# Hybrid streaming trunk on one core: the merge's weights split in two turns, in the middle of the second group's channel jobs

## The chip, the cores and the metric

One core of a Trainium2 chip runs the whole program. The metric is the device time of one execution in microseconds. The kernel before takes 2898.13 us in the median of three runs (2896.23 to 2900.97).

## The reference, cut to what matters

The reference is one step of an encoder layer over 2048 prompt rows and 8 x 16 sample rows, 17 tiles of 128 rows in all. Each row is normalised, h = RMSNorm(x), and multiplied by one wide input projection; its columns feed three branches (a gated convolution, a gated linear recurrence, a stick-breaking attention) and three sigmoid gates. Each branch's output is projected to 1024 columns, the three results are added with the gates as weights, and the sum goes through one output projection onto the residual.

```python
h = rms_norm(x, norm_g[l])
(a_x, a_b, a_c, a_z, g_q, g_f, g_i, g_z,
 s_q, s_k, s_v, s_z, m_a, m_b, m_c) = split_cols(h @ w_in[l])
...
y_a = o_a @ wb[:W_CONV]
y_b = o_b @ wb[W_CONV:W_CONV + W_HG]
y_c = o_c @ wb[W_CONV + W_HG:]
m = jax.nn.sigmoid(m_a) * y_a + jax.nn.sigmoid(m_b) * y_b + jax.nn.sigmoid(m_c) * y_c
return x + m @ w_out[l], conv_new, S_new.astype(x.dtype), k, v
```

Everything is float32.

## The kernel before, in words

Big products are done in three passes: a float32 operand is split into a rounded part and the rest (`split`, lines 173 to 176: a copy on ScalarE writes the rounded part, a subtraction on VectorE the rest), and high times high, high times low and low times high are added in PSUM. A weight that is used again is kept split in DRAM (`kept`), so that it is only loaded the next time (`wload`).

The rows go through the input projection in three groups (`GROUPS`: 5, 6 and 6 tiles), each of two chunks of up to three tiles. `group_jobs` makes a list of jobs for a group, 64 in the second and third. A channel job (`chan_job`, line 710) computes 128 output columns for a whole chunk, 24 matmuls of 384 columns, and hands the running program a turn after every six. A token job (`tok_job`, line 721) does 256 columns for each tile; keys, values and queries (`sk`, `sv`, `sq`) and the recurrence's `gi` are of this kind. `run_jobs` takes the jobs of a group in an order of pairs (job, chunk): in the second and third group it begins with jobs 0 and 1 on the first chunk, then jobs 0 and 1 on the second chunk, and goes on chunk by chunk; the position in this order is `at_`, from 0 to 127. Keys, values and queries take up the even jobs 2 to 12, that is positions up to 25.

Between the turns of a job `run_jobs` lets other work go on: the preparation of rows (`Prepare`), what is left of the norms of queries and keys (`run_late`), the recurrence (`hbg`) and the attention (`bg`). `Prepare` brings a tile of 128 rows into the transposed and split form that the matmuls read (`hx`), in steps: the load on the SyncE queue (line 607, 512 KB), the square with its sum on ScalarE (line 614), a power on GpSimd, the scaling on VectorE (line 619), and two turns of four transposes on TensorE (line 629), each followed by `split`. The tiles of rows have two buffers (`xt`) and a third for one of them (`xt3`). In the last group the sixth tile takes the buffer of the fourth, so its load has to wait until the fourth is transposed. `prep.advance()` does one step; `prep.chunk(ci)` does all steps up to the last tile of a chunk before a job on that chunk begins. Before the change, the first two jobs of every group (positions 0 and 1) make two steps in each of their turns, so the second chunk's rows are made while the first chunk's matmuls run.

The weights of the merge (12 pieces of the branch projections and 8 of the output projection) are split by the generator `split_merge_weights` while the second group runs, in 40 halves of 128 x 512. A half is a load into `mwx`, a split into `mwp` and a store to DRAM; each of the two tiles has one buffer. Before the change one of these three steps is made at the beginning of each position from 4 to 123.

What the Python code writes is not yet the order on the engines. The framework schedules the instructions and puts each into its engine's queue (TensorE, VectorE, ScalarE, GpSimd, and SyncE for all transfers); each engine takes its queue in order. An instruction can so be placed well ahead of others that the code writes earlier. A transfer also waits for the eighth transfer before it on the queue to be complete, since there are eight completion counters in turn.

Of the kernel before, what the change touches and what calls it, by code (L numbers as in the profile page):

```python
# [8 lines left out]
F32 = mybir.dt.float32  # L9
# [7 lines left out]
P = 128  # L17
# [81 lines left out]
def trunk(ctx: ExitStack, tc: tile.TileContext, x_prompt, x_sample, cache_conv, state_hgrn, cache_k, cache_v,  # L99
# [73 lines left out]
    def split(hi, lo, src, eng=None):  # L173

        first = nc.scalar.copy(hi, src)  # L175
        return first, (eng or nc.vector).tensor_tensor(lo, src, hi.bitcast(F32), ALU.subtract)  # L176
# [1097 lines left out]
    def branch_w(x, dp):  # L1274
        return ([wb[x * 512:(x + 1) * 512, dp * 256:(dp + 1) * 256].rearrange("(k p) m -> p k m", p=P)],
                ("branch", x, dp))

    def out_w(s):
        v = wo[:, s * 256:(s + 1) * 256].rearrange("(k p) m -> p k m", p=P)
        return [v[:, 0:4], v[:, 4:8]], ("out", s)  # L1280

    def split_merge_weights():

        mw = mwx.enter_context(tc.tile_pool(name="mw", bufs=1, side="right"))
        yield
        for pieces, key in [branch_w(x, dp) for x in range(3) for dp in range(4)] + [out_w(s) for s in range(4)]:
            for n, v in enumerate(pieces):
                kept[key, n] = dram.tile([P, 2, 1024], F32R, name=f"W{len(kept)}")
                a, b = v.shape[1], v.shape[2]
                for half in range(2):  # L1290
                    x = mw.tile([P, 512], F32, tag="mwx", name="mwx")
                    nc.sync.dma_start(x.rearrange("p (a b) -> p a b", b=b), v[:, half * a // 2:(half + 1) * a // 2])
                    yield
                    w = mw.tile([P, 2, 512], F32R, tag="mwp", name="mwp")
                    split(w[:, 0], w[:, 1], x)
                    yield
                    nc.sync.dma_start(kept[key, n][:, :, half * 512:(half + 1) * 512].bitcast(F32), w.bitcast(F32))
                    yield

    splitting = split_merge_weights()  # L1300

    def run_jobs(g, jobs):
# [13 lines left out]
        for at_, (i, ci) in enumerate(order):  # L1316
            weights(i)
            if g or at_:
                weights(i + 1)
            if g == 1 and 4 <= at_ < len(order) - 4:  # L1320
                next(splitting, None)
            if not g and at_ == 0:
                prep.advance()
            if not g and at_ == 2:

                with tc.issue_after(rstd_at[0].ins), tc.issue_after(prep.last[1].ins):
                    build_vectors()
                    build_hist()
                    build_rev()
                    build_bound()  # L1330
                    build_masks()
                    build_selectors()
            hT = prep.chunk(ci) if g or at_ > 1 else lambda ti, ci=ci: prep.tile(ci, ti)
            left = len(order) - at_
            if left == 5 and g + 1 < len(GROUPS):
                nxt = Prepare(g + 1)
            for cost in jobs[i][1](ws[i], ci, hT):
                if at_ < 2:
                    prep.advance()
                    prep.advance()  # L1340
                if nxt and (left <= 2 or nxt.ready < 0 and len(nxt.xt) < 3 or left <= 3 and not nxt.scaled):
                    nxt.advance()
                run_late(cost)
                hbg.run(cost * RATE_H)
                bg.run(cost * RATES[g] * jobs[i][2])
            if ci == 0 and g < len(GROUPS) - 1:
                wkeep(ws[i], jobs[i][0][1])
# [164 lines left out]
```

## Time and profile before

| | |
|---|---|
| median of 3 runs | 2898.13 us |
| profiled execution | 2896.27 us |
| its span | 2894.6 us |
| TensorE matmul busy | 2864.3 us, 99% of the span |
| VectorE, ScalarE, GpSimd busy | 1547.5, 1025.5, 317.0 us |
| second group begins | about 588 us |
| third group begins | about 1355 us |
| splits of the merge's weights | 584.0 to 1090.3 us |

The span is what lies between the first and the last instruction of the execution. A matmul counts as busy until its modelled end, and matmuls overlap, so the busy share of TensorE hides short delays; a delay is read from the start of one matmul to the start of the next. In rows of the timeline the bracket at the end gives the idle time of the engine before the instruction and what ended it. In rows of windows the columns are the window, its length, then the busy time and the number of instructions of TensorE's matmuls, its weight loads, VectorE, ScalarE and GpSimd, then the granted clock of TensorE (1.00 is 2.4 GHz, 0.50 is 1.2 GHz), the share of the transfer engines and the rate in GB/s.

### The profile page before, as it was taken

Reading aid. Unit: us, or ns where it says so; the run is one execution under the profiler, and the core shown is the slowest. Engines: PE = TensorE matmul, PEld = TensorE weight load, DVE = VectorE, ACT = ScalarE, POOL = GpSimd, SP = SyncE. Lnnn points to the kernel's source line nnn. Section 1 sums busy time; section 2 is a strip of 40 time slices with the busy share of each in tenths; the row PEclk is TensorE's granted clock in tenths of the full one; section 3 lists DMA queues with packets and bytes.
Section 4 is the critical chain, followed back from the end, with each engine's and each line's share of the span. In section 5 each row is a group of like instructions: output and inputs, shape, how many; then the busy total and the mean of one; then the engine's idle time right before and its main releaser. Section 6 shows DMA issues by size and latency. Waiting matters only on the chain.

```text
span 2894.6 us, 51726 instructions
## 1 busy us (share of the span) xinstructions
PE 2864.3 (99%) x19511; PEld 2671.5 (92%) x19511; DVE 1547.5 (53%) x3304; ACT 1025.5 (35%) x2391; POOL 317.0 (11%) x787
## 2 busy tenths in 40 slices
PE   9999999999999999999999999999999999999999
PEld 9999999989899999999999999999988888788888
DVE  5454645642334351526534757547475875867743
ACT  4333222242333332213334444434433444444420
POOL 3100000110100000001322111010110111110100
PEclk9999999999999999999999999999999999999999
DMA  8987767788777786446776454444446877878876
GB/s 306 310 262 241 242 219 246 245 266 289 247 246 255 258 262 202 152 138 185 218 231 206 140 178 131 161 139 150 146 138 222 293 241 233 262 251 265 271 251 223
DMA packets 367403, 645.57 MB, mean 223 GB/s; under 512 B 32969, under 2 KB 243746, under 8 KB 336434
## 3 DMA queue, kind: packets, MB, share of 16 engines
q1 hardware_dynamic: 367154, 642.26, 67.7%
q8 instruction: 155, 2.54, 0.4%
q14 instruction: 94, 0.77, 0.1%
HBM read 444.97 MB, written 197.17 MB: 222 GB/s over the span
## 4 chain that ended last, share of the span: by engine, by line
PE 73%; DMA 3%; DVE 3%; issue 1%; ACT 1%; POOL 1%; SPq 0%; ACTq 0%; DVEq 0%; POOLq 0%
PE acc L710 31%; PE acc L1420 10%; PE acc L721 8%; PE acc L1451 7%; PE pv L359 4%; PE tp L310 4%; PE z L330 2%; PE z L329 2%; DMA mwx<-in_w_branch_dram 1%; PE z L1040 1%; PE tp L458 1%; DMA mwx<-in_w_out_dram 1%; PE pv L522 1%; DMA GM<-gm 0%; PE z L476 0%
## 5 line engine op out<-in xcount | busy, mean ns | idle before, releaser
L710 PE MATMUL acc<-hx,w 128*128 128x384 f32 (+1 forms) x6816 | 1254.3, 333 | 0.1
L710 PEld LDWEIGHTS acc<-hx,w 128*128 128x128 f32 x6816 | 1107.4, 188 | 22.1 <-issue 15.2
L721 PE MATMUL acc<-w,hx 128*128 128x256 f32 x2544 | 330.3, 285 | 2.9 <-ACT kn L815 1.3
L342 DVE TENSOR_TENSOR_SCAN pr<-snb,carry 128x513 f32<-128x513 f32 x192 | 246.5, 1284 | 152.2 <-ACT snb L333 150.6
L721 PEld LDWEIGHTS acc<-w,hx 128*128 128x128 f32 x2544 | 312.4, 189 | 6.0 <-ACT kn L815 2.2
L311 ACT COPY aT<-tp 128x512 f32<-128x512 f32 (+2 forms) x320 | 167.7, 525 | 370.4 <-PE tp L310 357.5
L710 PE MATMUL acc<-hx,wst 128*128 128x384 f32 x1248 | 247.3, 344 | 0.0
L1420 PE MATMUL acc<-o,w 128*128 128x512 f32 (+2 forms) x1080 | 234.6, 363 | 1.1 <-DMA o<-OX 1.1
L333 ACT ACTIVATE snb<-z 128x512 f32<-128x512 f32 (+2 forms) x320 | 172.4, 539 | 144.3 <-PE z L330 140.7
L710 PEld LDWEIGHTS acc<-hx,wst 128*128 128x128 f32 x1248 | 215.5, 188 | 6.4 <-issue 3.7
L1420 PEld LDWEIGHTS acc<-o,w 128*128 128x128 f32 x1080 | 184.9, 188 | 33.0 <-issue 4.5
L347 DVE TENSOR_TENSOR sp<-sp,pr 128x512 f32<-128x512 f32 (+2 forms) x320 | 195.4, 611 | 26.7 <-DVE pr L342 1.0
L342 DVE TENSOR_TENSOR_SCAN pr<-snb,one 128x129 f32<-128x129 f32 (+3 forms) x128 | 114.5, 895 | 126.4 <-POOL snb L338 126.1
L310 PE MATMUL tp<-idf,sp 128*128 128x128 f32 x1088 | 171.3, 273 | 2.6 <-ACT aT L311 1.6
L335 ACT ACTIVATE sp<-z 128x512 f32<-128x512 f32 (+2 forms) x320 | 171.4, 536 | 0.0
L1451 PE MATMUL acc<-w,mh 128*128 128x256 f32 x816 | 160.5, 284 | 0.0
L310 PEld LDWEIGHTS tp<-idf,sp 128*128 128x128 f32 x1088 | 131.9, 141 | 19.6 <-issue 4.4
L176 DVE TENSOR_TENSOR w<-wst,w 128x1024 fp32r<-128x1024 f32 x72 | 88.1, 1224 | 106.3 <-ACT w L175 106.2
L1174 ACT ACTIVATE gm<-acc 128x384 f32<-128x384 f32 (+1 forms) x144 | 68.3, 474 | 213.8 <-PE acc L710 181.3
L1451 PEld LDWEIGHTS acc<-w,mh 128*128 128x128 f32 x816 | 130.7, 188 | 5.8 <-issue 4.2
L329 PE MATMUL z<-Kt,Q 128*128 128x512 f32 (+2 forms) x320 | 129.2, 404 | 0.4 <-ACT sp L335 0.2
L359 PE MATMUL pv<-aT,Vt 128*64 128x512 f32 (+3 forms) x640 | 128.1, 535 | 0.0
(302 smaller groups left out, 3581.5 us busy)
## 6 DMA issues: line engine op xcount, KB each, us to landing
w<-W SPq DMA_DIRECT2D x168, 1024.0 KB, 6.3
W<-w SPq DMA_DIRECT2D x72, 1024.0 KB, 5.0
wst<-W SPq DMA_DIRECT2D x112, 512.0 KB, 5.0
wst<-in_w_in_dram SPq DMA_DIRECT2D x72, 512.0 KB, 6.0
GM<-gm SPq DMA_DIRECT2D x120, 192.0 KB, 4.1
W<-mwp SPq DMA_DIRECT2D x40, 512.0 KB, 4.3
Kt<-KT SPq DMA_DIRECT2D x160, 128.0 KB, 3.9
o<-OX SPq DMA_DIRECT2D x72, 256.0 KB, 4.7
```

What stands on the lines that cost most here:

```text
L310: nc.tensor.transpose(tp[:, j * P:(j + 1) * P], sp[:, j * P:(j + 1) * P], idf)
L311: nc.scalar.copy(aT[:, e, 0:nb, i * P:(i + 1) * P], tp[:, :w].rearrange("p (b q) -> p b q", q=P))
L329: nc.tensor.matmul(z[:, :w], Q1[:, i * P:(i + 1) * P], Kt[:, :w], start=True, stop=False)
L333: nc.scalar.activation(sn[:, 512 - w:512], z[:, :w], AF.Sigmoid, scale=-0.125)
L335: nc.scalar.activation(sp[:, :w], z[:, :w], AF.Sigmoid, scale=0.125)
L342: nc.vector.tensor_tensor_scan(pr[:, 512 - w:513][:, ::-1], s_in, s_in, one if diag else carry[e][i], ALU.mult, ALU.bypass)
L347: nc.vector.tensor_tensor(sp[:, :w], sp[:, :w], pr[:, 513 - w:513], ALU.mult)
L359: nc.tensor.matmul(pv[64 * e:64 * e + 64, c0:n], Vt[:, j, e], aT[:, e, j, c0:n], start=first and j == 0, stop=last and j == nb - 1, skip_g ...
L710: nc.tensor.matmul(acc[:, :n], w[0][a][:, k], hT[b][:, k, :n], start=k == 0 and i == 0, stop=k == KB - 1 and i == 2)
L721: nc.tensor.matmul(acc[:, :256], hT[b][:, k, ti * P:(ti + 1) * P], w[k // 4][a][:, k % 4], start=k == 0 and i == 0, stop=k == KB - 1 and i ...
L1420: nc.tensor.matmul(acc[:, :n], w[0][a][:, k, dd * P:(dd + 1) * P], box[x][b][:, k, sl], start=k == 0 and i == 0, stop=k == 3 and i == 2)
L1451: nc.tensor.matmul(acc[:, :256], box["l" if b else "h"][:, k, ti * P:(ti + 1) * P], w[k // 4][a][:, k % 4], start=k == 0 and i == 0, stop= ...
```

## The change

The generator now makes a half in two turns: the first stores the half split before and loads the next one, the second splits. `run_jobs` calls it no longer at the beginning of a position but behind the second turn of a channel job (`jobs[i][2] == 1.0`) of the second group, from position 26 on, which is behind the jobs of keys, values and queries. There are 96 such places for 80 turns and the last store. One line beside it changes too: the two steps of `prep.advance()` in each turn of positions 0 and 1 are now made in the first group alone (`and not g`).

```diff
--- before.py
+++ after.py
@@ -1283,19 +1283,26 @@
 
         mw = mwx.enter_context(tc.tile_pool(name="mw", bufs=1, side="right"))
         yield
+        halves = []
         for pieces, key in [branch_w(x, dp) for x in range(3) for dp in range(4)] + [out_w(s) for s in range(4)]:
             for n, v in enumerate(pieces):
                 kept[key, n] = dram.tile([P, 2, 1024], F32R, name=f"W{len(kept)}")
-                a, b = v.shape[1], v.shape[2]
-                for half in range(2):
-                    x = mw.tile([P, 512], F32, tag="mwx", name="mwx")
-                    nc.sync.dma_start(x.rearrange("p (a b) -> p a b", b=b), v[:, half * a // 2:(half + 1) * a // 2])
-                    yield
-                    w = mw.tile([P, 2, 512], F32R, tag="mwp", name="mwp")
-                    split(w[:, 0], w[:, 1], x)
-                    yield
-                    nc.sync.dma_start(kept[key, n][:, :, half * 512:(half + 1) * 512].bitcast(F32), w.bitcast(F32))
-                    yield
+                a = v.shape[1] // 2
+                halves += [(v[:, half * a:(half + 1) * a], kept[key, n][:, :, half * 512:(half + 1) * 512])
+                           for half in range(2)]
+        made = None
+        for src, dst in halves + [(None, None)]:
+            if made:
+                nc.sync.dma_start(made[0].bitcast(F32), made[1].bitcast(F32))
+            if src is None:
+                return
+            x = mw.tile([P, 512], F32, tag="mwx", name="mwx")
+            nc.sync.dma_start(x.rearrange("p (a b) -> p a b", b=src.shape[2]), src)
+            yield
+            w = mw.tile([P, 2, 512], F32R, tag="mwp", name="mwp")
+            split(w[:, 0], w[:, 1], x)
+            made = (dst, w)
+            yield
 
     splitting = split_merge_weights()
 
@@ -1317,8 +1324,8 @@
             weights(i)
             if g or at_:
                 weights(i + 1)
-            if g == 1 and 4 <= at_ < len(order) - 4:
-                next(splitting, None)
+
+            extra = g == 1 and 26 <= at_ < len(order) - 2 and jobs[i][2] == 1.0
             if not g and at_ == 0:
                 prep.advance()
             if not g and at_ == 2:
@@ -1334,8 +1341,10 @@
             left = len(order) - at_
             if left == 5 and g + 1 < len(GROUPS):
                 nxt = Prepare(g + 1)
-            for cost in jobs[i][1](ws[i], ci, hT):
-                if at_ < 2:
+            for turn_, cost in enumerate(jobs[i][1](ws[i], ci, hT)):
+                if extra and turn_ == 1:
+                    next(splitting, None)
+                if at_ < 2 and not g:
                     prep.advance()
                     prep.advance()
                 if nxt and (left <= 2 or nxt.ready < 0 and len(nxt.xt) < 3 or left <= 3 and not nxt.scaled):
```

What this does to the queues shows at three places. The first is TensorE at the beginning of the third group, where the second chunk's rows (tiles `xt_15317`, `xt_15376` and a last one, 15472 before and 15631 now) are transposed; `acc_15458` and `acc_15598` (15553 now) are the first two jobs on the first chunk, `acc_15669` is the first job on the second chunk, and `z` are scores of the attention's first heads. Before:

```order
L710 MATMUL acc_15458<-hx_15272,w_15454 128x384 x6
L629 MATMUL tp_15465<-idf_79,xt_15317 128x128 x4
L710 MATMUL acc_15458<-hx_15272,w_15454 128x384 x12
L629 MATMUL tp_15535<-idf_79,xt_15376 128x128 x4
L710 MATMUL acc_15458<-hx_15272,w_15454 128x384
L629 MATMUL tp_15548<-idf_79,xt_15376 128x128 x4
L710 MATMUL acc_15458<-hx_15272,w_15454 128x384 x5
L710 MATMUL acc_15598<-hx_15272,w_15456 128x384 x16
L629 MATMUL tp_15555<-idf_79,xt_15472 128x128 x4
L629 MATMUL tp_15581<-idf_79,xt_15472 128x128
```

Now:

```order
L710 MATMUL acc_15553<-hx_15272,w_15456 128x384 x3
L629 MATMUL tp_15624<-idf_79,xt_15317 128x128 x4
L629 MATMUL tp_15641<-idf_79,xt_15376 128x128 x4
L329 MATMUL z_15607<-Kt_15482,Q1_15476 128x128
L330 MATMUL z_15607<-Kt_15482,Q2_15477 128x128
L329 MATMUL z_15686<-Kt_15482,Q1_15476 128x256
L629 MATMUL tp_15648<-idf_79,xt_15376 128x128 x4
L330 MATMUL z_15686<-Kt_15482,Q2_15477 128x256
L329 MATMUL z_15716<-Kt_15482,Q1_15476 128x384
L330 MATMUL z_15716<-Kt_15482,Q2_15477 128x384
L629 MATMUL tp_15655<-idf_79,xt_15631 128x128 x4
L629 MATMUL tp_15662<-idf_79,xt_15631 128x128 x4
```

The transposes stood between matmuls of the first chunk; now they stand behind the last of them, together, with scores between, and directly ahead of the second chunk's first matmuls.

The second place is SyncE's queue in the same stretch. Before, the last tile of rows was loaded behind the first of the attention's transfers:

```order
L1175 DMA GM_77<-gm_15431 128x384
L281 DMA Q1_15481<-QT_73 64x512
L282 DMA Q2_15482<-QT_73 64x512
L607 DMA xt_15472<-in_x_prompt_dram 128x1024
L281 DMA Q1_15481<-QT_73 64x512
L282 DMA Q2_15482<-QT_73 64x512
L287 DMA Kt_15487<-KT_72 64x512 x2
L291 DMA Vt_15490<-VV_74 128x4x128
```

Now its load stands behind three sets of them, the last of which is for the third head, and behind the store of a gate (`gm_15620`):

```order
L281 DMA Q1_15594<-QT_73 64x512
L282 DMA Q2_15595<-QT_73 64x512
L281 DMA Q1_15594<-QT_73 64x512
L282 DMA Q2_15595<-QT_73 64x512
L287 DMA Kt_15600<-KT_72 64x512 x2
L291 DMA Vt_15603<-VV_74 128x4x128
L320 DMA ot_15605<-SZ_76 128x512
L1183 DMA SZ_76<-gm_15620 128x384
L607 DMA xt_15631<-in_x_prompt_dram 128x1024
```

The load has moved back by twenty places in the queue.

The third place is ScalarE at the beginning of the second group. `hx_6983` is the second chunk's rows, `xt_15094` and `xt_15109` are the first rows of the third group, which the scheduler fetches as soon as a buffer is free, `mwp` are halves of the merge's weights, and `sq` and `kn` further down belong to the first job of keys. Before:

```order
L175 CAST hx_6983<-tp_6998 128x4x128
L175 CAST hx_6983<-tp_7039 128x4x128
L175 CAST hx_6983<-tp_7046 128x4x128
L614 ACTIVATE junk_6975,ssq_6976<-xt3_6973 128x1024
L459 COPY kt_7059<-tp_7062 128x4x128
L1133 ACTIVATE gm_7094<-acc_6991 128x384
L175 CAST hx_6983<-tp_7074 128x4x128
L175 CAST hx_6983<-tp_7081 128x4x128
L175 CAST mwp_7635<-mwx_7573 128x512
```

Now:

```order
L175 CAST hx_6983<-tp_7120 128x4x128
L175 CAST hx_6983<-tp_7128 128x4x128
L175 CAST hx_6983<-tp_7135 128x4x128
L175 CAST mwp_9691<-mwx_9639 128x512
L175 CAST hx_6983<-tp_7142 128x4x128
L614 ACTIVATE junk_15096,ssq_15097<-xt_15094 128x1024
L175 CAST hx_6983<-tp_7149 128x4x128
L614 ACTIVATE junk_15111,ssq_15112<-xt_15109 128x1024
```

The square of `xt_15094` stood behind all casts of the second chunk's rows; now it stands ahead of the last of them. In VectorE's queue the scaling of `xt_15094` has likewise come to stand ahead of the last subtraction of `hx_6983`. A little later, in the first job of keys, ScalarE's queue had:

```order
L813 ACTIVATE sq_7315<-acc_7290 128x256
L815 COPY kn_7317<-acc_7290 128x256
L175 CAST mwp_8247<-mwx_8152 128x512
L813 ACTIVATE sq_7353<-acc_7325 128x256
L815 COPY kn_7355<-acc_7325 128x256
L614 ACTIVATE junk_15137,ssq_15138<-xt3_15135 128x1024
```

and has now:

```order
L813 ACTIVATE sq_7312<-acc_7287 128x256
L815 COPY kn_7314<-acc_7287 128x256
L175 CAST mwp_9914<-mwx_9842 128x512
L813 ACTIVATE sq_7350<-acc_7322 128x256
L815 COPY kn_7352<-acc_7322 128x256
```

A cast of the merge's weights (`mwp`) stands behind the second `kn` of the keys' job in both, although the code now writes it only from position 26 on; the square of `xt3_15135`, a row tile of the third group, has left this stretch. Behind these two stretches, at the beginnings of the second and the third group, the queues of all five engines read the same before and after.

## Rows read from the trace of the kernel before

**Rows 1.** The page's busy times: time, share of the span and number of instructions of each engine.

```profile
PE 2864.3 (99%) x19511; PEld 2671.5 (92%) x19511; DVE 1547.5 (53%) x3304; ACT 1025.5 (35%) x2391; POOL 317.0 (11%) x787
```

**Rows 2.** Windows of 50 us in which TensorE is not busy throughout.

```profile
600.00:650.00 50.00, 46.14 (x359) 43.70 (x358) 23.66 (x43) 20.96 (x49) 10.69 (x20) 1.00 0.80 256
750.00:800.00 50.00, 44.99 (x360) 43.24 (x359) 18.07 (x42) 15.41 (x40) 10.82 (x18) 0.97 0.74 237
1350.00:1400.00 50.00, 46.68 (x330) 44.74 (x329) 30.50 (x59) 22.42 (x58) 16.68 (x34) 1.00 0.79 220
```

**Rows 3.** Who waited for whom, TensorE alone, 600 to 800 us: sum in us, times, longest.

```profile
PE hg L827 <- DVE kt L176: 7.1, 4, 3.0
PE acc L721 <- ACT kn L815: 1.3, 1, 1.3
PE tp L629 <- DVE xt L619: 0.8, 1, 0.8
```

**Rows 4.** The same for ScalarE, the wait for the merge's weights.

```profile
ACT mwp L175 <- DMA mwx<-in_w_branch_dram: 38.0, 14, 5.6
```

**Rows 5.** The casts of the merge's weights: duration in ns (least, median, greatest), first and last start.

```profile
L175 ACT CAST mwp<-mwx x40: 617/620/626, 584.0 to 1089.6; 128x512 fp32r<-128x512 f32 x40
```

**Rows 6.** Windows of 2 us behind two idle times of TensorE.

```profile
590.00:592.00 2.00, 0.92 (x5) 0.95 (x6) 1.53 (x5) 0.77 (x2) 0.00 (x0) 0.80 1.06 416
592.00:594.00 2.00, 2.00 (x9) 2.00 (x8) 0.46 (x2) 1.65 (x4) 0.74 (x2) 0.50 0.92 349
594.00:596.00 2.00, 2.00 (x11) 2.00 (x11) 2.00 (x3) 0.00 (x0) 0.00 (x0) 0.85 0.99 245
638.00:640.00 2.00, 0.00 (x0) 0.00 (x0) 0.77 (x2) 0.54 (x2) 1.08 (x2) 1.00 0.69 233
640.00:642.00 2.00, 1.53 (x10) 1.53 (x11) 0.74 (x3) 0.00 (x0) 1.08 (x2) 1.00 1.00 198
```

**Rows 7.** Timeline of TensorE at the beginning of the third group: start, duration, engine, line, operation, count, idle time before.

```profile
1354.79 1.29 PE L710 MATMUL acc<-hx,w 128*128 128x384 f32 x6
...
1365.29 0.74 PE L629 MATMUL tp<-idf,xt 128*128 128x128 f32 x5 [1.26 <-DVE xt L619]
1365.78 0.31 PE L329 MATMUL z<-Kt,Q 128*128 128x128 f32 x1
...
1368.06 0.33 PE L710 MATMUL acc<-hx,w 128*128 128x384 f32 x1
...
1369.02 2.36 PE L710 MATMUL acc<-hx,w 128*128 128x384 f32 x12
1371.21 0.38 PE L310 MATMUL tp<-idf,sp 128*128 128x128 f32 x2
```

**Rows 8.** Timeline of SyncE's queue in the same stretch; a duration is that of issuing.

```profile
1356.62 0.33 SPq L607 DMA_DIRECT2D xt<-in_x_prompt_dram  x1
...
1358.14 1.24 SPq L287 DMA_DIRECT2D Kt<-KT  x2
...
1368.02 0.45 SPq L281 DMA_DIRECT2D Q<-QT  x1
...
1370.43 1.23 SPq L287 DMA_DIRECT2D Kt<-KT  x2
...
1373.54 0.33 SPq L320 DMA_DIRECT2D ot<-SZ  x1
1374.01 3.02 SPq L1183 DMA_DIRECT2D SZ<-gm  x2
```

**Rows 9.** Transfers by line: count, KB each, median us from issue to landing.

```profile
Kt<-KT SPq DMA_DIRECT2D x160, 128.0 KB, 3.9
...
xt<-in_x_prompt_dram SPq DMA_DIRECT2D x16, 512.0 KB, 5.2
```

**Rows 10.** Transfers of row tiles, all 17: least, median and greatest time from issue to landing.

```profile
DMA to landing us min/median/max: 3.5/5.2/8.7
```

**Rows 11.** Timeline of ScalarE at the beginning of the third group: the square of the last row tile, and the cast of its first turn.

```profile
1361.76 1.06 ACT L614 ACTIVATE junk<-xt 128x1024 bf16<-128x1024 f32 x1 [0.81 <-DMA xt<-in_x_prompt_dram]
...
1365.95 0.59 ACT L175 CAST hx<-tp 128x512 fp32r<-128x512 f32 x1 [2.66 <-PE tp L629]
```

**Rows 12.** Timeline of VectorE there: the scaling of that tile, and the subtraction of its first turn.

```profile
1363.85 1.29 DVE L619 SCALAR_TENSOR_TENSOR xt<-xt,rr,g_bc 128x1024 f32<-128x1024 f32 x1 [2.18 <-POOL rr L234]
...
1366.57 0.69 DVE L176 TENSOR_TENSOR hx<-tp,hx 128x512 fp32r<-128x512 f32 x1 [0.96 <-ACT hx L175]
```

**Rows 13.** Timeline of TensorE at the beginning of the second group.

```profile
578.78 0.60 PE L629 MATMUL tp<-idf,xt 128*128 128x128 f32 x4
...
602.76 1.07 PE L629 MATMUL tp<-idf,xt 128*128 128x128 f32 x8 [0.81 <-DVE xt L619]
...
640.47 0.44 PE L827 MATMUL hg<-idf,kn 128*128 128x128 f32 x2 [2.99 <-DVE kt L176]
```

**Rows 14.** Timeline of VectorE there: the subtraction of one turn, the scaling of a row tile of the third group, and a subtraction for a key that TensorE waits for.

```profile
580.03 0.69 DVE L176 TENSOR_TENSOR hx<-tp,hx 128x512 fp32r<-128x512 f32 x1 [1.81 <-ACT hx L175]
...
631.36 1.28 DVE L619 SCALAR_TENSOR_TENSOR xt<-xt,rr,g_bc 128x1024 f32<-128x1024 f32 x1 [0.45 <-POOL rr L234]
...
640.00 0.41 DVE L176 TENSOR_TENSOR kt<-hg,kt 128x256 fp32r<-128x256 f32 x1
```

## The prediction

> **What bounds the kernel now.** I read the page's busy times first. TensorE is busy for 2864.3 of 2894.6 us, and no other engine for more than 53% [rows 1]. So the time is TensorE's work and the little that it waits; a change off TensorE counts only where TensorE waits, at once or later. I then cut the span into windows of 50 us to find where it does: 3.9 us between 600 and 650, 5.0 between 750 and 800, 3.3 between 1350 and 1400 [rows 2]. These are the beginnings of the second and the third group, and the second group's jobs of keys, values and queries. Who ends these waits comes next: between 600 and 800 us it is VectorE, four times with a subtraction for a key or query (7.1 us), once ScalarE with a copy of one (1.3), once a scaled row tile (0.8) [rows 3]. ScalarE itself waits 38.0 us in these 200 us for the loads of the merge's weights [rows 4], and each later copy of a key stands behind that in its queue. So at first sight the change aims at something that is there: with the splits gone from these jobs, up to 7.1 + 1.3 = 8.4 us of waits could go.
>
> The granted clock belongs to it. After the wait that ends at about 591 us it stood at 0.80, 0.50 and 0.85 in three windows of 2 us: in part of them TensorE ran at 1.2 GHz, and (0.20 + 0.50 + 0.15) x 2 = 1.7 us were lost. After the longer wait of 2.99 us that ends at 640.47 it stayed at 1.00 [rows 6, 13].
>
> **The splits themselves: 0 us.** Nothing is removed: 40 halves with 40 loads, casts, subtractions and stores, 620 ns a cast [rows 5]. What counts is where they stand in the queues, and the pieces of order on ScalarE show a split at the same place, behind the second key of the first job, though the code writes it twenty-two positions later. From there on all five queues read as before. So ScalarE's 38.0 us stay, and the 8.4 us with them. Were the splits really gone from these jobs, the gain would be at most 8.4 + 1.7 = 10 us; I take 0 and keep 10 as the end.
>
> **The preparation, third group: +12 us, and +1.7 for the clock.** The small line `and not g` does move things. Before, the second chunk's first matmul there began at 1369.02 + 6 x 0.183 = 1370.1 us (0.183 is 2.19 / 12, from 1369.02 to 1371.21) [rows 7]. Now the chain is:
> - The first chunk's matmuls run undisturbed from 1354.79. After 42 of them, at 1362.5, the first scores need a key tile; its issuing ended at 1359.4, and with 3.9 us to landing it is there at 1363.3 [rows 7 to 9]. The first head's scores take 1.6 us (1365.78 to 1368.4, less three transposes of the row tile and two matmuls), the six matmuls left 1.1. So the transposes begin at 1366.0.
> - The last row tile takes the fourth's buffer, free at 1366.5. But SyncE reaches its load only behind the third head's transfers and a gate's store. The first of these went out at 1368.02, as the first head's scores released a buffer; that release is now at about 1365.6. From it to the store took 6.0 us (1374.01), with waits for earlier transfers in it [rows 8]. So the load goes out at about 1372.0, against 1356.62 before.
> - 5.2 us to landing [rows 9]: 1377.2. From the start of the square to that of the scaling 2.1 us (1361.76 to 1363.85), from there to the transposes 1.4 (1365.29), from these to the end of the subtraction 2.0 (1367.26) [rows 7, 11, 12]. The first matmul with that part goes at 1382.7.
>
> That is 12.6 us later than 1370.1. In the meantime TensorE does three score products of the second head that came later before; they take about 0.8 of the 1.6 that four of the first head took. Nothing else covers the wait: behind the waiting transposes in TensorE's queue stand all matmuls of the second chunk. So +12. The trace does not show this wait, so it has bounds: with the least and the greatest landing (3.5 and 8.7) [rows 10] it is +10 and +15.5, and if SyncE finds its earlier transfers complete, 1.2 us less. I take 12, at the median. TensorE is then idle for about 7 us on end. I add 1.7 for the clock, as behind the wait at 591; the row at 640 says 0.
>
> The Trainium skill has a section for this ("TensorE: Matmul & The Clock Gate", HAM oscillation): a wait for a transfer between groups of matmuls lets the array fall back to half the clock, and what follows begins cold. The trace agrees behind one wait and not behind the other [rows 6]; by the rule the time is 2914, without it 2912.
>
> **The preparation, second group: +3 us.** Five turns of four transposes stood between matmuls; now they stand together behind the first chunk. With T as their start: one turn from its transposes to its subtraction's end took 1.94 us (578.78 to 580.03 + 0.69) [rows 13, 14]. There are two PSUM tiles, so the third turn starts at T + 1.9 and the fifth at T + 3.9; the fourth's subtraction, behind one on the merge's weights, ends at T + 5.2. The next twelve matmuls and a block of transposes need only that much, till T + 7.8. Then TensorE needs the fifth turn, whose cast is now behind the square of a row tile of the third group. That tile's load can start only when the first turn has freed its buffer, at T + 0.7, and lands at T + 5.9. The scaling starts 2.1 later, at T + 8.0, takes 1.3 [rows 14], and then comes the fifth subtraction: T + 10.0. TensorE's work in this time is 20 transposes (2.0), 13 matmuls (2.4) and 0.4, so it loses 5.2 us. Two things come off: the wait of 0.81 at 602.76 [rows 13], and the third row tile's square and scaling, which leave the first job of keys. The scaling took 1.28 us of VectorE at 631.36, in the queue ahead of the subtraction at 640.00 for which TensorE waited 2.99 [rows 13, 14]; I take off 1.2. That leaves 5.2 - 0.8 - 1.2 = 3. Bounds, by 3.5 and 8.7 to landing and all of the 2.99 or nothing saved there: -0.3 and +8.
>
> The Trainium skill speaks against this part of the change too ("Perfetto Trace Analysis", Optimization Strategy): phases with different limits gain from being interleaved. Before, the transposes were interleaved with matmuls and cost TensorE 0.81 us of waiting in the second group [rows 13]; the change takes this interleaving back, so by the rule the sum has the same sign.
>
> **The sum.** 0 + 12 + 1.7 + 3 = +16.7. The profiled execution took 2896.27 us, 1.7 more than its span; it is 1.9 below the median. 2896.27 + 16.7 = 2913.0, and from the median 2914.8. I say 2914.
>
> **The rivals.** First: the bunches are mostly covered. The load of the last tile goes out as soon as its buffer is free, at 1366.5, and lands in 3.5; then the chain ends 7.2 us sooner, the clock stays up as at 640 [rows 6], and the second group gives back 0.3: 12 - 7.2 - 0.3 = +4.5, from the median 2902.6. For it: other transfers between may have completed by then; against it: SyncE waited between these issues before [rows 8].
>
> Second, the other side: the splits do leave the jobs of keys, because the delays at the beginning put the merge's loads ahead of ScalarE's need. Then the 10 us of rows 3 and 6 go, and if the third group's bunch costs no more than +4, the time is 2898 - 10 + 4 = 2892; it decides where the bunch stays under 4.2. Against it: the loads are issued behind a key's store, so they keep their distance from the copies.
>
> Third: worse. Both bunches come at their upper ends, 15.5 and 8, with a fall of the clock in each (3.4): +27, or 2925. For it: DMA queues are full in both stretches (at least 0.79 of the engines' time) [rows 2].
>
> **How the numbers follow.** A measurement of this kernel tells about 0.2% from no change, 5.8 us: 2892.3 to 2903.9 is the same. My forecast (about 2905 to 2920) has 0.70, the first rival 0.15, the second 0.05, the third 0.10. The range of 8 in 10 is 2904 to 2923; it leaves out the second rival, most of the first and part of the third. Slower has 0.80 (forecast and third), the same 0.15, faster 0.05.
>
> **What would show it.** In the changed kernel's timeline the last row tile's load should go out at about 1372 us or later (counted with the shift of the second group), and TensorE should be idle for 6 to 9 us ahead of its transposes, ended by VectorE's scaling (line 619). In the second group two waits should stand ahead of and within the second chunk's first job, the second ended by a subtraction into `hx`. ScalarE's wait for the merge's weights between 600 and 800 us should stay near 38 us. The granted clock should fall behind the long wait. I am wrong if the load lands without TensorE waiting, if ScalarE's wait falls by more than half, or if the time comes from a stretch whose queues read the same.

## The result, and the profile after

The changed kernel takes 2916.39 us in the median of four runs (2911.80 to 2918.18), the kernel before 2899.42 beside it (2896.23 to 2900.97). The ratio is 1.0048, with a 95% interval of 1.0034 to 1.0061. It is slower by 0.5%, some 17 us. The profiled execution took 2916.38 us, with a span of 2914.6. Of all executions in this document one, of the last kernel below, took 12214 us, and it is counted nowhere.

The page's line of TensorE, which answers to [rows 1]:

```profile
PE 2867.8 (98%) x19511; PEld 2673.9 (92%) x19511; DVE 1548.1 (53%) x3304; ACT 1024.5 (35%) x2391; POOL 315.3 (11%) x787
```
TensorE is busy for 3.5 us more, with the same 19511 matmuls; some of them ran at the lower clock, as the windows below show. The other engines are busy as before. Two windows that answer to [rows 2], same columns:

```profile
600.00:650.00 50.00, 42.87 (x319) 39.73 (x319) 23.21 (x42) 19.13 (x44) 9.65 (x18) 0.93 0.76 248
1350.00:1400.00 50.00, 36.18 (x213) 33.45 (x212) 22.86 (x39) 19.77 (x49) 9.53 (x22) 0.86 0.57 173
```
In the second group's window TensorE is idle for 7.1 us where it was 3.9. Between 1350 and 1400 us it is idle for 13.8 us where it was 3.3, and the granted clock of that window is 0.86. The beginning of the third group, in TensorE's timeline (start, duration, engine, line, operation, count, idle time before), answers to [rows 7]:

```profile
1362.44 7.63 PE L710 MATMUL acc<-hx,w 128*128 128x384 f32 x42
...
1372.69 0.60 PE L629 MATMUL tp<-idf,xt 128*128 128x128 f32 x4
...
1377.75 0.66 PE L629 MATMUL tp<-idf,xt 128*128 128x128 f32 x4 [3.24 <-DVE hx L176]
...
1388.26 1.94 PE L629 MATMUL tp<-idf,xt 128*128 128x128 f32 x8 [9.39 <-DVE xt L619]
1390.02 2.69 PE L710 MATMUL acc<-hx,w 128*128 128x384 f32 x7
```
The transposes of the second chunk's rows stand together behind the 42 matmuls of the first chunk, as the order of the queues has it. The last eight of them waited 9.39 us for VectorE, which scaled the last row tile. Why it scaled so late is seen in SyncE's queue (against [rows 8]), in ScalarE's (against [rows 11]) and in VectorE's (against [rows 12]):

```profile
1379.83 0.38 SPq L607 DMA_DIRECT2D xt<-in_x_prompt_dram  x1
```
```profile
1384.74 1.06 ACT L614 ACTIVATE junk<-xt 128x1024 bf16<-128x1024 f32 x1 [5.04 <-DMA xt<-in_x_prompt_dram]
```
```profile
1386.83 1.28 DVE L619 SCALAR_TENSOR_TENSOR xt<-xt,rr,g_bc 128x1024 f32<-128x1024 f32 x1 [5.24 <-POOL rr L234]
```
The load of that tile was issued 17.39 us behind the group's first matmul; before it was 1.83 us (1356.62 less 1354.79). ScalarE is idle for 5.04 us until it lands and the square begins, the scaling comes 2.09 us later, the transposes 1.43 us behind that. What TensorE did next is in the windows of 2 us (the column before the last two is the granted clock):

```profile
1388.00:1390.00 2.00, 1.74 (x8) 1.57 (x8) 0.12 (x1) 0.59 (x1) 0.00 (x0) 0.50 0.04 8
1390.00:1392.00 2.00, 2.00 (x7) 1.75 (x7) 1.38 (x2) 0.59 (x1) 0.00 (x0) 0.50 0.00 0
1392.00:1394.00 2.00, 2.00 (x12) 1.90 (x11) 0.00 (x0) 0.66 (x2) 0.24 (x1) 0.83 0.00 0
```
It came out of the idle time at 1.2 GHz and was back at 2.4 GHz within the window from 1392 us: 2.2 us lost (half of 1.74 + 2.00, and 0.17 x 2). The whole distance from the first chunk's first matmul to the second chunk's is 27.58 us (1362.44 to 1390.02), and was 15.33 (1354.79 to 1370.12, six matmuls behind 1369.02).

The second group's beginning, TensorE (against [rows 13]), ScalarE and VectorE (against [rows 14]):

```profile
601.86 1.03 PE L629 MATMUL tp<-idf,xt 128*128 128x128 f32 x8
603.86 1.25 PE L629 MATMUL tp<-idf,xt 128*128 128x128 f32 x8 [0.96 <-DVE hx L176]
605.92 0.66 PE L629 MATMUL tp<-idf,xt 128*128 128x128 f32 x4 [0.80 <-DVE hx L176]
...
611.65 1.15 PE L710 MATMUL acc<-hx,w 128*128 128x384 f32 x5 [1.72 <-DVE hx L176]
```
```profile
607.61 1.06 ACT L614 ACTIVATE junk<-xt 128x1024 bf16<-128x1024 f32 x1 [1.47 <-DMA xt<-in_x_prompt_dram]
...
608.67 0.57 ACT L175 CAST hx<-tp 128x512 fp32r<-128x512 f32 x1
```
```profile
609.71 1.28 DVE L619 SCALAR_TENSOR_TENSOR xt<-xt,rr,g_bc 128x1024 f32<-128x1024 f32 x1 [2.65 <-POOL rr L234]
610.91 0.68 DVE L176 TENSOR_TENSOR hx<-tp,hx 128x512 fp32r<-128x512 f32 x1
```
Here the transposes begin at 601.86, and the matmuls that need their last part stand at 611.65. The part's cast stands behind a square that waited for its row tile, its subtraction behind that tile's scaling.

Last, the waits for the merge's weights. ScalarE between 600 and 800 us (against [rows 4]), and the casts in the whole run (against [rows 5]):

```profile
ACT mwp L175 <- DMA mwx<-in_w_branch_dram: 45.3, 13, 5.6
```
```profile
L175 ACT CAST mwp<-mwx x40: 617/620/624, 584.8 to 1096.8; 128x512 fp32r<-128x512 f32 x40
```
The casts run from 585 to 1097 us, as before the change, and wait no less (45.3 us against 38.0). The splits have not left the jobs of keys, values and queries, although they are written behind them.

One thing does not fit yet. The third group's first matmul is 7.65 us later than before (1362.44 against 1354.79), of which the second group's bunch was to bring 3. The rest arose in a stretch in which all queues read the same.

### The profile page after: what moved, and what is told of

It is laid out like the page before. It is cut to its first block, busy times and chain, and to the rows that moved or that the text cites. A ratio compares the mean times of both kernels' runs of the same rounds, so it can differ in the third digit from the quotient of the medians.

```text
span 2914.6 us, 51721 instructions
## 1 busy us (share of the span) xinstructions
PE 2867.8 (98%) x19511; PEld 2673.9 (92%) x19511; DVE 1548.1 (53%) x3304; ACT 1024.5 (35%) x2391; POOL 315.3 (11%) x787
## 4 chain that ended last, share of the span: by engine, by line
PE 74%; DMA 4%; DVE 2%; ACT 1%; issue 1%; POOL 1%; SPq 0%; ACTq 0%; DVEq 0%; POOLq 0%
PE acc L710 31%; PE acc L1429 10%; PE acc L721 8%; PE acc L1460 7%; PE pv L359 4%; PE tp L310 4%; PE z L330 2%; PE z L329 2%; DMA mwx<-in_w_branch_dram 2%; PE z L1040 1%; PE tp L458 1%; PE pv L522 1%; PE z L476 0%; POOL rr L234 0%; DMA GM<-gm 0%
```

## The experiments

My theory: the dropped steps of the preparation make the whole difference, through a late load in the third group and less in the second, and moving the split in the code makes none. Theory B: the splits in the middle of channel jobs bring the part that did not fit.

### The two edits apart, and the two groups apart

Four kernels, compared with the kernel before in the same session (2899.78 us, median of 23 runs). The first has only the second edit:

```diff
-                if at_ < 2:
+                if at_ < 2 and not g:
```

> The kernel before, and only the second edit: positions 0 and 1 of the second and third group no longer make steps of the preparation. The splits are written as before. Theory A (the dropped steps cost, the split's new place costs nothing): +17 us over before, 2914 to 2919 us, like the changed kernel, of which 12 in the third group. Theory B (the 5.9 us that the changed kernel lost between 618 us and the third group, behind its first bunch, come from the splits in the middle of channel jobs): about +11 us, 2908 to 2912.

Measured: 2916.04 us, ratio 1.0058 (1.0046 to 1.0070). The one line alone makes the whole loss.

The second is the changed kernel with that line taken back:

```diff
-                if at_ < 2 and not g:
+                if at_ < 2:
```

> The changed kernel with the two steps of the preparation back in positions 0 and 1 of every group, so that only the splits are moved. Theory A: within 3 us of before, 2896 to 2902 us. Theory B: +5 to +6 us, 2903 to 2906. A third (the splits' waits do leave the jobs of keys and values, rival 2 of the prediction): -7 to -10 us, 2889 to 2893.

Measured: 2900.77 us, ratio 0.9998 (0.9987 to 1.0010): nothing. Theory B falls here, and so does the third, that the splits leave those jobs.

The third and the fourth are the changed kernel with the steps back in the second group, and with the steps back in the third:

```diff
-                if at_ < 2 and not g:
+                if at_ < 2 and g != 2:
...
+                if at_ < 2 and g != 1:
```

> The changed kernel with the steps back in the second group: they are dropped in the third group alone. Theory A: +12 to +13 us over before, 2911 to 2913 us; the second chunk of the third group starts some 27 us behind the first one where it was 15.3 us. If the loss of the third group hangs on the second group's (another arrival of its loads), less: +5 to +8.

> The changed kernel with the steps back in the third group: they are dropped in the second group alone. Theory A: the second group's bunch with what follows it, +4 to +8 us over before, 2903 to 2907 us, by the trace of the changed kernel (third group's first matmul 7.65 us later); +3 by the prediction's own sum, 2902. If the 7.65 us come from the splits and not from the bunch: as much as the run with the splits alone.

Measured: dropped in the third group alone 2912.81 us, ratio 1.0036 (1.0024 to 1.0049), +13.0; dropped in the second alone 2901.63, ratio 1.0006 (0.9996 to 1.0017), +1.9. Together that is 14.9, against 16.3 with the line alone.

The fourth also answers the part that did not fit. Up to the third group its queues hold the same instructions in the same order as the changed kernel's, yet its third group begins 7.26 us sooner. The table follows the first matmul of the keys' first job (617.13), three instructions of ScalarE and the third group's first matmul through single profiled executions, each as a difference to the kernel before:

| before, us | changed | splits alone | dropped in second alone | held back | no transfers |
|---|---|---|---|---|---|
| 617.13 | +1.74 | -0.73 | +3.75 | -2.35 | -1.47 |
| 703.96 | +5.14 | +0.47 | +6.66 | -6.13 | +9.97 |
| 818.12 | +2.96 | +0.19 | +2.34 | -13.45 | +2.65 |
| 963.94 | +8.65 | +1.14 | +1.07 | -15.54 | +0.10 |
| 1354.79 | +7.65 | +0.06 | +0.39 | -16.03 | -2.11 |

(The last two columns are of runs below.) The changed kernel's execution lost 5.7 us between 818 and 964 where the other gained 1.3. It lost most of them here, on ScalarE and then TensorE:

```profile
897.21 0.62 ACT L175 CAST mwp<-mwx 128x512 fp32r<-128x512 f32 x1 [4.52 <-DMA mwx<-in_w_branch_dram]
897.74 0.37 ACT L1053 COPY ktm<-tp 128x256 f32<-128x256 f32 x1
```
```profile
898.16 0.79 PE L1089 MATMUL tp<-vg,ktm 128*128 128x128 f32 x2 [3.66 <-ACT ktm L1053]
```
A cast of the merge's weights waited 4.52 us for its load, the copy `ktm` of the recurrence stood behind it, and TensorE waited 3.66 us for `ktm`. In the execution of the fourth kernel the same instructions met no such wait. So 7.65 was a measure of one execution, not of the change. The kernel with the steps dropped in the third group alone, which has no bunch in the second, begins its third group 4.07 us later than before (1358.86).

### The late load by itself

The changed kernel, but in the third group the steps go on until the sixth tile's load is issued:

```diff
-                if at_ < 2 and not g:
+                if at_ < 2 and (not g or g == 2 and 5 not in prep.xt):
```

> The changed kernel, but in the third group positions 0 and 1 make steps until the sixth tile's load has been issued, and none from there on: the fourth tile's transposes and the last load stand where they stood before, the fifth and sixth tile are transposed together ahead of position 2. Theory A (the late load is what costs in the third group): -8 to -11 us against the changed kernel, 2905 to 2908 us. Theory B (standing together is what costs, with or without the load): 0 to -4 us, 2912 to 2916.

Measured: 2907.44 us, ratio to before 1.0025 (1.0012 to 1.0038), 9.0 us under the changed kernel's median. SyncE and TensorE in that run:

```profile
1360.80 0.33 SPq L607 DMA_DIRECT2D xt<-in_x_prompt_dram  x1
```
```profile
1358.98 1.29 PE L710 MATMUL acc<-hx,w 128*128 128x384 f32 x6
...
1376.77 0.69 PE L629 MATMUL tp<-idf,xt 128*128 128x128 f32 x2 [3.59 <-DVE hx L176]
...
1379.62 0.52 PE L710 MATMUL acc<-hx,w 128*128 128x384 f32 x1
```
The load goes out 1.82 us behind the group's first matmul, as before the change. The 9.39 us are gone; what is left is a wait of 3.59 us for the subtraction of an earlier turn, and 20.64 us between the two chunks' first matmuls. Of the 12.25 us more, the load made 6.9 and standing together 5.3 (scores that were pulled ahead count in it, and so does a fall of the clock: it is 0.50 from 1376 to 1380 us, and the matmul at 1379.62 takes 0.52 us where one took 0.33 in [rows 7]). From the third group's first matmul to the end of the span it is 1552.2 us in the changed kernel, 1543.7 here, and 1539.8 before: by that measure 8.4 and 3.9. Theory A holds: the load is the larger part, though standing together is not free.

### What the splits cost where they stand

If moving the code does not move the splits, how much was there to win? The first try leaves out all loads but one, so that no cast can wait for a load:

```diff
-                    x = mw.tile([P, 512], F32, tag="mwx", name="mwx")
-                    nc.sync.dma_start(x.rearrange("p (a b) -> p a b", b=b), v[:, half * a // 2:(half + 1) * a // 2])
+                    if x is None:
+                        x = mw.tile([P, 512], F32, tag="mwx", name="mwx")
+                        nc.sync.dma_start(x.rearrange("p (a b) -> p a b", b=b), v[:, half * a // 2:(half + 1) * a // 2])
```

> The kernel before, with only the first of the 40 loads into mwx: every split reads the first half, so the kept weights of the merge are wrong and no cast waits for a transfer; casts, subtractions and stores stay. It is a bound on what the casts' waits for mwx cost before. If they hold the keys' and values' jobs as the prediction's end of -10 has it: 2886 to 2892 us, and less scatter. If they lie beside other work: 2897 to 2902.

Measured: 2893.85 us, ratio 0.9974 (0.9964 to 0.9985), against 2900.4 for before. It fell between the two answers because it was no clean bound. ScalarE's waits in the second group:

```profile
ACT mwp L175 <- DMA W<-mwp: 89.6, 36, 5.6
```
With the loads gone, the casts waited for the stores of the one buffer `mwp` instead, 89.6 us in all against 101.0 for the loads before. The wait was renamed, not removed. Between 600 and 800 us it even came to 41.9 us, against 38.0 before [rows 4], so this run does not show what the waits cost there.

The second try does what the change says. Each load is tied behind the transfer of weights written last (`fetched[0]` is what `wload` issued), the steps of the preparation stay:

```diff
-            nc.sync.dma_start(x.rearrange("p (a b) -> p a b", b=src.shape[2]), src)
+            with tc.issue_after(fetched[0].ins):
+                nc.sync.dma_start(x.rearrange("p (a b) -> p a b", b=src.shape[2]), src)
```

> The run with the splits alone, and each load into mwx is tied behind the transfer of the weights that was written last, so that loads and casts really stand behind the jobs of keys, values and queries; the steps of the preparation as before. Rival 2 of the prediction: -7 to -10 us against before, 2889 to 2893. If the casts' waits only change place and hold the channel jobs and the recurrence there: 2896 to 2902.

Measured: 2881.89 us, ratio 0.9934 (0.9916 to 0.9952): 18.5 us faster than before, and the best kernel of this study. Its five runs lie within 0.8 us, where the 29 of the kernel before lay between 2891.9 and 2911.8. Its casts, ScalarE's waits for them from 575 to 1340 us, all waits of TensorE in the same stretch, and two of the windows that answer to [rows 2]:

```profile
L175 ACT CAST mwp<-mwx x40: 610/621/624, 790.3 to 1231.5; 128x512 fp32r<-128x512 f32 x40
```
```profile
ACT mwp L175 <- DMA mwx<-in_w_branch_dram: 50.8, 20, 5.9
...
ACT mwp L175 <- DMA mwx<-in_w_out_dram: 20.7, 8, 4.4
```
```profile
PE tp L1114 <- DVE hx L176: 2.7, 2, 1.7
PE tp L459 <- DVE hx L176: 0.6, 1, 0.6
PE tp L1090 <- ACT ktm L1054: 0.5, 1, 0.5
PE z L1041 <- ACT sps L486: 0.2, 1, 0.2
```
```profile
600.00:650.00 50.00, 50.00 (x399) 48.15 (x398) 20.96 (x41) 19.44 (x45) 11.40 (x20) 1.00 0.70 222
750.00:800.00 50.00, 50.00 (x432) 48.70 (x434) 15.87 (x36) 15.77 (x42) 8.42 (x14) 1.00 0.73 231
```
TensorE is now busy throughout both windows. The casts begin at 790 us, behind the queries. They still wait 71.5 us for their loads, and TensorE hardly notices: 4.0 us of waits in the whole second group, and none for a key or query (`kt`, `kn`). Before, these three waits from 575 to 1340 us came on top of those in [rows 3]:

```profile
PE tp L1089 <- ACT ktm L1053: 2.5, 3, 1.2
PE tp L629 <- DVE hx L176: 2.1, 1, 2.1
...
PE z L1040 <- DVE sc L1005: 1.0, 2, 0.6
```
Together that is 14.8 us before and 4.0 now. In the table 2.35 us are won ahead of the keys' first job, 3.8 from there to 704 us, and another 7.3 up to 818 us. Part of this is the clock: before, it fell after the wait at 591 us (1.7 us, [rows 6]) and again between 750 and 800 us (0.97 of 50 us, that is 1.5, [rows 2]), and in this run it fell at neither place. The waits and the two falls make 14.0 of the 16.0 us.

A third try gives the loads a buffer more (the low part is written in place to make room):

```diff
+            x = mw.tile([P, 512], F32, tag="mwx", name="mwx", bufs=2)
...
-                    split(w[:, 0], w[:, 1], x)
+            split(room.bitcast(F32R), x.bitcast(F32R), x)
```

> The kernel before, with two buffers for mwx, each load one half ahead of its split, the low part written in place (so that the room stays the same) and the two parts stored apart: 40 more stores of 256 KB instead of 512 KB ones, the same bytes. If the casts' waits for mwx cost time: as the run with one load, 2886 to 2893 us, but for what 40 more transfers in SyncE's queue cost (up to +3). If not: 2897 to 2903.

Measured: 2906.95 us, ratio 1.0016 (1.0003 to 1.0030): slower, which neither answer had. ScalarE's waits for the splits in that run:

```profile
ACT mwp L175 <- DMA W<-mwp: 65.1, 21, 6.4
...
ACT mwp L175 <- DMA mwx<-in_w_branch_dram: 24.4, 10, 4.1
...
ACT mwp L175 <- DMA mwx<-in_w_out_dram: 17.8, 7, 4.1
```
The waits for loads fell from 101.0 to 42.2 us, and the casts waited 65.1 us for stores besides: 107.3 us in all, no less than before.

The fourth takes nearly all transfers away (the loads as in the first try), and was meant to leave the casts' and subtractions' own work alone:

```diff
+                first = one is None
+                if first:
+                    one = dram.tile([P, 2, 1024], F32R, name=f"W{len(kept)}")
+                kept[key, n] = one
...
+                    if first:
+                        nc.sync.dma_start(kept[key, n][:, :, half * 512:(half + 1) * 512].bitcast(F32), w.bitcast(F32))
```

> The kernel before with one load into mwx and two stores of mwp; the other 39 loads and 38 stores are left out, and all pieces of the merge's weights read the one that was stored, so the output projections are wrong. The 40 casts and 40 subtractions stay; with nothing to wait for, the schedule brings them forward, closer together, into the first jobs of keys. If the casts' waits for transfers (in the run with one load for the stores, 50.1 us of them) hold the jobs: as the run with the loads held back, 2879 to 2885 us. If the casts' and subtractions' own work on ScalarE and VectorE in those jobs is what costs: 2890 to 2900.

Measured: 2895.59 us, ratio 0.9985 (0.9974 to 0.9995). The casts, their largest wait, and two of TensorE's waits:

```profile
L175 ACT CAST mwp<-mwx x40: 610/620/635, 582.7 to 678.7; 128x512 fp32r<-128x512 f32 x40
```
```profile
ACT mwp L175 <- DVE mwp L176: 30.4, 29, 2.2
```
```profile
639.26 1.33 PE L710 MATMUL acc<-hx,w 128*128 128x384 f32 x6 [3.33 <-ACT kn L815]
642.54 0.69 PE L827 MATMUL hg<-idf,kn 128*128 128x128 f32 x2 [1.95 <-DVE kt L176]
```
All 40 halves are made by 682 us, 38 of them from 605 us on. Those jobs cost 10.0 us more than before (the table at 703.96), and TensorE waits there for `kn` and `kt` though hardly a cast waits for a transfer. But this is no clean bound either: the casts now wait 30.4 us for the subtraction of the split before, which frees the one buffer `mwp`. The stretch from 704 to 818 us, now without splits, gives back 7.3 (9.97 to 2.65), as much as with the loads held back, and the recurrence 2.5. So splits among the jobs of keys cost TensorE time even without waits for transfers; whether it is their work or the wait for the buffer is not shown. How the 18.5 us divide between work, waits and the traffic of transfers is not settled either: the number of splits in a job changed with it.

### The change as it is written down

With the loads held back, and the steps dropped as in the changed kernel:

```diff
-                if at_ < 2:
+                if at_ < 2 and not g:
```

> The run with the loads held back, and the steps of the preparation dropped in the second and third group as in the changed kernel: the change with its splits really behind the jobs of keys, values and queries. If the parts add up: 2882 + 13 (third group) + 2 (second group) = 2897 us, 2894 to 2899, just below before. If the second group's bunch costs more without the splits beside it, or the clock falls behind it: 2900 to 2904.

Measured: 2898.78 us in the median of eleven executions, ratio 0.9995 (0.9984 to 1.0006), 16.9 us over the kernel with the loads held back. Its third group, and the first matmul of the third group with the loads held back:

```profile
1343.25 7.64 PE L711 MATMUL acc<-hx,w 128*128 128x384 f32 x42
...
1358.55 1.11 PE L630 MATMUL tp<-idf,xt 128*128 128x128 f32 x4 [3.24 <-DVE hx L176]
...
1370.12 1.94 PE L630 MATMUL tp<-idf,xt 128*128 128x128 f32 x8 [9.61 <-DVE xt L620]
1371.88 2.69 PE L711 MATMUL acc<-hx,w 128*128 128x384 f32 x7
```
```profile
1338.76 1.29 PE L711 MATMUL acc<-hx,w 128*128 128x384 f32 x6
```
The same wait stands here with 9.61 us, and 28.63 us lie between the chunks. The third group begins 4.5 us later than with the steps (1343.25 against 1338.76), of which 2.7 had come by the keys' first job (617.45 against 614.78). That is the price of the second group's bunch in this pair of executions.

## Why the prediction was right

2914 was forecast, with a range of 2904 to 2923, and 2916.4 was measured: slower, at the place and by the mechanism forecast.

**The splits, 0 us: right.** ScalarE's wait was to stay near 38 us and measured 45.3; the run with the splits alone differs by 1.0 us, within its interval. Where the prediction said that the queues read as before behind the two beginnings, that held for the whole change.

**What could be won, at most 10 us: too small.** Rival 2 put the splits' leaving at 10 us; held back, they gave 18.5. The step that failed is the bound: it summed the waits of TensorE for keys and queries between 600 and 800 us (8.4) and one fall of the clock (1.7). It left out the wait of 2.1 us at 591, the second fall that [rows 2] show with 0.97 (1.5 us), and 3.5 us of waits in the recurrence behind 850 us, where TensorE is not busy throughout either, though [rows 2] do not list that window. The table has 13.5 us by 818 and 2 more in the recurrence. The rival's condition was rightly given 0.05, its price was not.

**The third group, +12 and +1.7 for the clock: right, with two steps that offset each other.** The load was to go out at about 1372.0 and the second group's shift, that is 1379.65, and went out at 1379.83. On the way there the first scores did not wait for their key tile, so that the third head's transfers began at 1372.43 instead of 1373.25 (1365.6 and the shift); from these to the gate's store it then took 7.0 us (to 1379.41) instead of 6.0. That the load went out within 0.2 us of the forecast is thus in part luck. From there to the first matmul of the second chunk 10.7 us were forecast (1372.0 to 1382.7), 10.2 came. The distance between the chunks was to grow by 12.6 and grew by 12.25. The clock fell, and cost 2.2 us, some of it inside that distance (the eight transposes took 1.94 us). From the first matmul to the end the group grew by 12.35 us; the run that drops the steps there alone has +13.0. The sum of 13.7 is thus a little too high; part of the fall lies in the 12.25 already.

The page "TensorE: Matmul & The Clock Gate" of the Trainium skill (HAM oscillation) was cited with 2914 by its rule and 2912 without. Behind this wait the trace agrees: the clock stood at 0.50. Behind shorter ones the traces show both (below). The page "Perfetto Trace Analysis" of the Trainium skill (Optimization Strategy) says that interleaving phases with different limits may improve performance; the prediction took from it that taking an interleaving back costs time, and the trace agrees, with 12.25 us in one group.

**The second group, +3 us: right in size, by two terms that offset each other.** The chain came out as written: the row tile's square at T + 5.75 (its landing forecast at T + 5.9), its scaling at T + 7.85 (8.0), the matmuls behind the last subtraction at T + 9.8 (10.0). The first matmul of the keys' first job stands at 618.87 to 620.88 us in the four kernels with the bunch (changed, line alone, second alone, early load) and at 615.98 to 617.13 in three without (before, splits alone, third alone): 3.4 us later in the mean, where 5.2 - 0.8 = 4.4 were forecast by then. The 1.2 us taken off for the keys' first job did not come: TensorE waits 2.6 to 3.5 us there in the four, and 1.9 to 3.0 in the three. By whole executions the bunch alone measured +1.9 (interval -1.2 to +4.9), with the loads held back +4.5 in the trace. Of the 7.65 of the profiled execution 5.9 arose behind the bunch, where the queues read the same; the prediction had named that as a sign of being wrong. Over the executions it is scatter: the third group begins 0.4 us later than before in one kernel with the bunch and 4.1 later in one without.

**The rivals.** The first (2902.6) fell with the late load; and the kernel with the early load shows what such a cover would have brought: +7.0 us (interval +3.5 to +11.0), where the rival had +4.5. The third (2925) needed both upper ends, and neither came.

## What to carry to other kernels

Where a framework schedules, a step that is moved in the code need not move on the engine: these 40 splits stayed where they were until their loads were tied. Read the queues, and look for the line beside it that does move something. The steps of preparation that stood between matmuls hid their loads; put together, they showed the last load with 9.39 us of waiting. The sum of an engine's waits does not tell what they cost: 71.5 us of ScalarE's waits left TensorE 4.0 us of its own in one place, and among the jobs of keys and queries the same splits, with 38.0 us of waits, went with a kernel 18.5 us slower. And an instruction whose transfer is taken away may wait for the next thing: here for stores, then for a buffer.

## What was not expected of the hardware

**The clock behind the same wait.** TensorE waits 2.1 to 2.2 us for the same subtraction at about 591 us in six of the kernels. In the changed kernel and in the kernel with the steps dropped in the second alone:

```profile
590.99 1.06 PE L629 MATMUL tp<-idf,xt 128*128 128x128 f32 x8 [2.17 <-DVE hx L176]
```
```profile
591.92 1.94 PE L629 MATMUL tp<-idf,xt 128*128 128x128 f32 x8 [2.16 <-DVE hx L176]
```
The same eight transposes took 1.06 us in the one and 1.94 in the other. In the changed kernel the granted clock stayed at 1.00 there (against [rows 6]), and fell later, around two waits of 1.64 and 1.82 us:

```profile
592.00:594.00 2.00, 2.00 (x14) 1.96 (x13) 1.29 (x3) 1.78 (x4) 0.13 (x1) 1.00 0.87 172
...
642.00:644.00 2.00, 1.17 (x5) 1.17 (x6) 1.08 (x3) 0.00 (x0) 0.73 (x2) 0.50 1.13 248
```
Before the change it fell at 591 and stayed up behind a wait of 2.99 us. And behind a wait of 3.24 us in the third group four transposes took 0.66 us in the changed kernel and 1.11 in the last one (both lines stand above). In these runs a single wait of 2 to 3.2 us does not tell whether the clock falls. Behind the wait of 8.8 to 9.9 us in the third group the same eight transposes took 1.94 us in all four kernels that have it.

**The scatter.** Executions of one program differ by up to 20 us (before, 29 runs). With the splits out of the jobs of keys, values and queries five differ by 0.8 us. I read the scatter as the casts' waits for transfers in those jobs, sometimes with a fall of the clock. That is not shown: no run varied it alone, and in the last kernel the splits are out of those jobs too, yet its eleven executions lie between 2894.6 and 2900.8 us.
